# Edge tiles of a dilated attention with whole 128-row blocks

## The chip, the cores and the metric

The kernel runs on one core of one Trainium2 chip. The metric is the device time of one execution in microseconds (us); less is better. The time before is 2080.05 us, the median of three runs (2075.96 to 2084.55).

## The reference, cut to what matters

The layer normalises x (2048 tokens of 1024 channels), projects it, runs a state-space branch and an attention branch beside each other, gates both and adds the result to x. The change lies in the attention alone. Each of 8 heads attends in three patterns (window, dilation) = (128, 1), (512, 4), (2048, 16), always 64 keys to either side on its own sub-sequence, and the patterns are merged by their log-sum-exp:

```python
valid = (jnp.abs(ki - qi) <= half) & (ki >= 0) & (ki < n)
s = jnp.einsum('nhbqd,nhbkd->nhbqk', qb, kb) * (1.0 / math.sqrt(D))
s = jnp.where(valid, s, NEG_INF)
m = jnp.max(s, axis=-1, keepdims=True)
p = jnp.where(valid, jnp.exp(s - m), 0.0)
den = jnp.sum(p, axis=-1, keepdims=True)
o = jnp.einsum('nhbqk,nhbkd->nhbqd', p, vb) / den
```

Keys before the first or after the last token of a sub-sequence do not exist, so a query tile at either edge has fewer keys than one in the middle.

## The kernel before

Three phases follow each other. `phase_a` (to about 1068 us) normalises, projects and runs the state space. `phase_b` (about 1094 to 1701 us) runs the attention, and beside it the remaining projections and the gated linear unit as filler. `phase_c` merges the branches and does the output projection.

`phase_b` (L1299) walks 80 steps, made by `attn_steps` (L934): for each of 4 head pairs hp, the patterns p = 1, 0, 2 in that order; p = 1 and p = 0 have 8 steps of two query tiles, p = 2 has 4 steps of four. A step is a two-head piece of work in three stages, and the loop issues stage one of step i, stage two of step i-1 and stage three of step i-2, with filler from `run` (L1278) after each:

- `attn_scores` (L950) loads q and v at the first step of a quad (four tiles) by DMA from the POOL queue (from SP for the first two quads), makes the scores S in PSUM, adds the mask into P in SBUF while it finds the row minimum (VectorE, L1003), and takes the exponential of P in place (ScalarE, L1007). P is a tile of a pool with two buffers a head.
- `attn_turn` (L1010) transposes P on TensorE, four blocks a head into one PSUM tile `pp` (L1019), and copies `pp` to SBUF tiles `t` (L1030 ScalarE, L1032 VectorE). `pp` has two buffers.
- `attn_values` (L1036) multiplies each transposed block with its block of v into `po` (L1048). At the end of a quad `po` is copied out (L1059), and after p = 2 `attn_merge` (L1078) joins the three patterns through small DMAs and the products `ab` (L1117 to L1122).

A query tile in the middle has 256 keys, two blocks of 128. The first and the last tile of a sub-sequence have 192: one block of 64 and one of 128. `q_tiles` (L880) lists them. For p = 1 every step holds one such tile (sub-sequences of four tiles, two a step); for p = 0 the first and the last of eight steps do; p = 2 has none. So 40 of the 80 steps are edge steps, ten a head pair. In an edge step the 64-key block is transposed into 64 rows of `pp`, copied apart from the three others (two copies a head, dealt to ScalarE and VectorE in turn by `self.ev_`), and multiplied as a matmul over 64 rows. Each product with v is two matmul records in the trace, so a step has sixteen of `po`, of which an edge step has four with 64 rows.

The kernel is written with a planner that sets the order of the instructions on each engine from a simulated timeline; dependencies alone bind it, so the order in the trace is not the order of the source.

Of the kernel before, what the change touches and what calls it, by code (L numbers as in the profile page):

```python
# [9 lines left out]
F32 = mybir.dt.float32  # L10
F32R = mybir.dt.float32r
I32 = mybir.dt.int32
AF = mybir.ActivationFunctionType
# [26 lines left out]
class Kern:  # L40
# [862 lines left out]
    def attn_setup(self, base, ctx, pctx):  # L903
        ap, R = self.pool, dict(ctx=ctx, side="right")
        self.op = ap("op", ctx=base, side="right")
        self.kp = ap("kp", **R)
        self.qa = ap("qa", bufs=2, **R)
        self.vp = ap("vp", bufs=2, **R)
        self.aw = ap("aw", bufs=2, **R)
        mp = ap("mk", **R)  # L910
        self.mg = ap("mg", **R)

        self.kh = [self.kp.tile([128, 2048], F32R, name=f"kh{h}") for h in range(2)]
        self.kl = [self.kp.tile([128, 2048], F32R, name=f"kl{h}") for h in range(2)]
        self.mk = {}
        for n in ("m2", "m1", "m3"):
            t = mp.tile(list(self.ins[n].shape), F32, name=n)
            self.nc.sync.dma_start(t, self.ins[n])
            self.mk[n] = t
        self.pS = ap("pS", bufs=3, space=PSUM, ctx=pctx)  # L920
        self.pT = ap("pT", bufs=2, space=PSUM, ctx=pctx)
        self.pO = ap("pO", bufs=1, space=PSUM, ctx=pctx)
        self.ev_ = 0
        self.O = [self.op.tile([128, 2048], F32, name=f"o{p}", tag=f"o{p}") for p in range(2)] + [None]

    def k_load(self, hp, r):
# [23 lines left out]
    def attn_scores(self, x):  # L950
        nc, mm, R, C = self.nc, self.mm, 2048, 512
        hp, p, quad, per, g = x["hp"], x["p"], x["quad"], x["per"], x["group"]
        tiles = self.tiles[p]
        if x["sub"] == 0:
            late = hp > 0 or p != 1 or quad > 1

            g["q"] = [self.qa.tile([128, 512], F32R, name=f"q{h}") for h in range(2)]
            for h in range(2):
                o = (8 * p + 2 * hp + h) * 2 * 64 * R + 512 * quad
                (nc.gpsimd if late else nc.sync).dma_start(f(g["q"][h]), at(self.QT, o, [[R, 128], [1, 512]]))  # L960

            v = g["v"] = self.vp.tile([128, 5, 128], F32, name="v")
            c0 = 128 * hp
            if p == 2:
                (nc.gpsimd if late else nc.sync).dma_start(v[:, :4], at(self.V, 512 * quad * C + c0, [[4 * C, 128], [C, 4], [1, 128]]))
            else:
                run = 8 if p == 0 else 32
                base, m0 = (0, 4 * quad) if p == 0 else (512 * quad, 0)
                for m in range(m0, m0 + 5):
                    j0, j1 = max(run * m - run // 2, 0), min(run * m + run // 2, 128)  # L970
                    rows = [[512 * C, 4], [C, 4 * (j1 - j0)]] if p == 0 else [[C, 4 * (j1 - j0)]]
                    (nc.gpsimd if late else nc.sync).dma_start(v[:(16 if p == 0 else 4) * (j1 - j0), m - m0],  # L972
                                                               at(self.V, (base + 4 * j0) * C + c0, rows + [[1, 128]]))
            if p == 2:
                self.st[2] = self.aw.tile([128, 2, 2, 4], F32, name="st2", bufs=3)
            elif quad == 0:
                self.st[p] = self.aw.tile([128, 2, 2, 16], F32, name="st")
        q, kh, kl = g["q"], self.kh, self.kl
        st = x["st"] = self.st[p]
        w = 512 // per  # L980
        S = [self.pS.tile([128, per, w], F32, name="s") for h in range(2)]
        x["P"] = [self.aw.tile([128, per, w], F32, name=f"p{h}") for h in range(2)]
        for i, t in enumerate(x["idx"]):
            qs = slice(128 * (t % 4), 128 * (t % 4) + 128)
            for h in range(2):
                c = 0
                for ko, kd, kn, _ in tiles[t][0]:
                    o_ = S[h][:, i, c:c + kn]
                    mm(o_, q[h][:, qs], vw(kh[h], ko, kd), start=True, stop=False)
                    mm(o_, q[h][:, qs], vw(kl[h], ko, kd), start=False, stop=True)  # L990
                    c += kn
        for h in range(2):
            for i, t in enumerate(x["idx"]):
                nk, mask = tiles[t][2], self.mk[tiles[t][1]]
                c = (t, 4 * (t % 4) + t // 4, t % 4)[p]
                least, o = st[:, 0, h, c:c + 1], 0
                for _, kd, kn, m0 in tiles[t][0]:
                    pt, sc, mk = x["P"][h][:, i, o:o + kn], S[h][:, i, o:o + kn], mask[:, m0:m0 + kn]
                    if kn == 64:
                        pt, sc, mk = vw(pt, 0, [[16, 4], [1, 16]]), vw(sc, 0, [[16, 4], [1, 16]]), vw(mask, m0, [[32, 4], [1, 16]])  # L1000
                    elif len(tiles[t][0]) == 2:
                        mk = mask[:, (m0 + 127) // 128 * 128:][:, :128]
                    self.marks["dve"] = nc.vector.tensor_tensor_reduce(pt, sc, mk, op0=OP.add, op1=OP.min, scale=-0.125,  # L1003
                                                                       scalar=least if o else 3e38, accum_out=least)
                    o += kn
                pt = x["P"][h][:, i, :nk]
                self.marks["act"] = nc.scalar.activation(pt, pt, AF.Exp, bias=st[:, 0, h, c:c + 1], scale=-1.0,  # L1007
                                                         accum_out=st[:, 1, h, c:c + 1])

    def attn_turn(self, x):  # L1010

        nc, tiles = self.nc, self.tiles[x["p"]]
        x["blocks"] = blocks = [(i, b, b * tiles[t][3][0][1], vt, n) for i, t in enumerate(x["idx"])
                                for b, (vt, n) in enumerate(tiles[t][3])]
        x["T"] = []
        for h in range(2):
            pp = self.pT.tile([128, 4, 128], F32, name="pp")
            for c, (i, b, o, vt, n) in enumerate(blocks):
                self.tr(pp[:n, c], x["P"][h][:, i, o:o + n], self.ident)  # L1019
            ts = self.aw.tile([128, 4, 128], F32, name=f"t{h}")  # L1020
            rows = [y[4] for y in blocks]
            c = 0
            while c < 4:
                e = c
                while e < 4 and rows[e] == rows[c]:
                    e += 1
                o_, i_ = ts[:rows[c], c:e], pp[:rows[c], c:e]
                self.ev_ += 1
                if self.ev_ % 2:
                    nc.scalar.activation(o_, i_, AF.Copy)  # L1030
                else:
                    nc.vector.tensor_copy(o_, i_)  # L1032
                c = e
            x["T"].append(ts)

    def attn_values(self, x):  # L1036
        nc, mm, R = self.nc, self.mm, 2048
        hp, p, quad, per, g = x["hp"], x["p"], x["quad"], x["per"], x["group"]
        tiles = self.tiles[p]
        if x["sub"] == 0:  # L1040
            g["po"] = self.pO.tile([128, 4, 128], F32, name="po")
            if p == 2:
                g["o2"] = self.op.tile([128, 512], F32, name="o2", bufs=3)
        po, v, O = g["po"], g["v"], self.O
        for c, (i, b, o, vt, n) in enumerate(x["blocks"]):
            last = b == len(tiles[x["idx"][i]][3]) - 1
            for h in range(2):
                mm(po[64 * h:64 * h + 64, per * x["sub"] + i], v[:n, vt, 64 * h:64 * h + 64], x["T"][h][:n, c],  # L1048
                   start=b == 0, stop=last)
        if x["sub"] < 4 // per - 1:  # L1050
            return
        if p == 0:
            o_ = vw(O[0], 32 * quad, [[8, 4], [128, 16], [1, 8]])
        elif p == 1:
            o_ = vw(O[1], 512 * quad, [[32, 4], [128, 4], [1, 32]])
        else:
            o_ = g["o2"].rearrange("p (a j) -> p a j", a=4)
        i_ = po if p == 2 else po.rearrange("p m (s j) -> p m s j", s=16 if p == 0 else 4)
        (nc.scalar.copy if quad % 2 else nc.vector.tensor_copy)(o_, i_)  # L1059
        if p == 2:  # L1060
            self.merges.append(self.attn_merge(hp, quad, x["st"], g["o2"]))
        elif quad == 3:
            self.merges.append(self.attn_stats(hp, p, x["st"]))
# [435 lines left out]
```

## Time and profile before

| | before |
|---|---|
| median of three runs | 2080.05 us |
| the profiled execution | 2084.98 us |
| its span, first to last instruction | 2083.2 us |
| TensorE matmul busy | 1975.6 us, 95% |
| TensorE weight load busy | 1764.6 us, 85% |
| VectorE busy | 1292.2 us, 62% |
| ScalarE busy | 725.7 us, 35% |
| GpSimd busy | 826.8 us, 40% |
| mean granted TensorE clock | 0.974 |
| chain of work that ended last | TensorE 59%, VectorE 16%, DMA 13% |

The profiled execution took 1.9 us more than its span and 0.24% more than the median. PE is TensorE's matmuls and PEld its weight loads, DVE is VectorE, ACT ScalarE, POOL GpSimd, SP SyncE. A form such as `128*64` on PE gives the rows and the columns of the array that the instruction uses. Matmuls are pipelined and their ends are modelled, so the distance between two starts says more of TensorE's pace than the duration of one.

### The profile page before, as it was taken

Reading aid. Unit: us, or ns where it says so; the run is one execution under the profiler, and the core shown is the slowest. Engines: PE = TensorE matmul, PEld = TensorE weight load, DVE = VectorE, ACT = ScalarE, POOL = GpSimd, SP = SyncE. Lnnn points to the kernel's source line nnn. Section 1 sums busy time; section 2 is a strip of 40 time slices with the busy share of each in tenths; the row PEclk is TensorE's granted clock in tenths of the full one; section 3 lists DMA queues with packets and bytes.
Section 4 is the critical chain, followed back from the end, with each engine's and each line's share of the span. In section 5 each row is a group of like instructions: output and inputs, shape, how many; then the busy total and the mean of one; then the engine's idle time right before and its main releaser. Section 6 shows DMA issues by size and latency. Waiting matters only on the chain.

```text
span 2083.2 us, 37578 instructions
## 1 busy us (share of the span) xinstructions
PE 1975.6 (95%) x13612; PEld 1764.6 (85%) x13612; DVE 1292.2 (62%) x3312; ACT 725.7 (35%) x1829; POOL 826.8 (40%) x1088
## 2 busy tenths in 40 slices
PE   6899999999999999899989999998998978999999
PEld 6788899998788889899977877876887978899997
DVE  8867575978566778587755455455567655433432
ACT  4221343333232343233326544554655632100110
POOL 4310464538636654475442346346345222000000
PEclk9999999999999999999999999999998998999999
DMA  5632464445533444634474465566676547433332
GB/s 192 195 100 73 126 198 147 121 120 158 166 109 114 153 144 141 178 114 133 130 230 138 154 180 165 166 178 179 208 204 179 161 134 233 147 114 115 117 111 76
DMA packets 272059, 312.54 MB, mean 150 GB/s; under 512 B 86594, under 2 KB 182226, under 8 KB 271874
## 3 DMA queue, kind: packets, MB, share of 16 engines
q1 hardware_dynamic: 250914, 260.39, 41.8%
q0 software_dynamic: 20960, 49.76, 8.1%
q8 instruction: 107, 1.75, 0.3%
q14 instruction: 78, 0.64, 0.1%
HBM read 202.12 MB, written 105.71 MB: 148 GB/s over the span
## 4 chain that ended last, share of the span: by engine, by line
PE 59%; DVE 16%; DMA 13%; SPq 4%; issue 3%; POOL 3%; ACT 2%; DVEq 0%; ACTq 0%; POOLq 0%
PE acc L53 39%; PE po L53 12%; PE s L53 3%; PE pp L56 3%; DMA raw<-in_w_in 2%; DVE wlo L311 2%; DMA ab<-AL 2%; SPq L513 1%; DVE zs L843 1%; DMA AL<-e 1%; DMA ACTA<-fth 1%; DVE zs L841 1%; DMA s<-ST 1%; PE y L53 1%; SPq L1111 1%
## 5 line engine op out<-in xcount | busy, mean ns | idle before, releaser
L53 PE MATMUL acc<-xh,whi 128*128 128x512 f32 (+1 forms) x960 | 376.7, 393 | 17.8 <-DVE xsc L379 8.3
L53 PE MATMUL acc<-whi,xh 128*128 128x256 f32 x1280 | 368.2, 288 | 2.9 <-ACT qr L451 2.1
L53 PE MATMUL acc<-xl,whi 128*128 128x512 f32 (+1 forms) x960 | 367.9, 384 | 1.1 <-DVE xl L208 1.1
L53 PE MATMUL acc<-xh,wlo 128*128 128x512 f32 (+1 forms) x960 | 367.3, 384 | 0.0
L53 PE MATMUL acc<-whi,xl 128*128 128x256 f32 x1280 | 364.7, 285 | 1.9 <-POOL xl L263 1.6
L53 PE MATMUL acc<-wlo,xh 128*128 128x256 f32 x1280 | 364.7, 285 | 0.0
L53 PEld LDWEIGHTS acc<-whi,xh 128*128 128x128 f32 x1280 | 247.9, 194 | 5.6 <-ACT qr L451 2.4
L53 PEld LDWEIGHTS acc<-whi,xl 128*128 128x128 f32 x1280 | 247.9, 194 | 2.5 <-POOL xl L263 1.9
L53 PEld LDWEIGHTS acc<-wlo,xh 128*128 128x128 f32 x1280 | 248.1, 194 | 0.0
L53 PEld LDWEIGHTS acc<-xh,whi 128*128 128x128 f32 x960 | 184.9, 193 | 54.0 <-issue 10.9
L1007 ACT ACTIVATE p<-p,st 128x256 f32<-128x256 f32 (+2 forms) x384 | 172.8, 452 | 143.6 <-DVE st L1003 143.2
L311 DVE TENSOR_TENSOR wlo<-raw,whi 128x512 fp32r<-128x512 f32 x168 | 151.2, 918 | 110.9 <-ACT whi L310 110.1
L53 PEld LDWEIGHTS acc<-xh,wlo 128*128 128x128 f32 x960 | 184.9, 193 | 33.7 <-issue 0.5
L53 PEld LDWEIGHTS acc<-xl,whi 128*128 128x128 f32 x960 | 185.4, 193 | 29.4 <-DVE xl L208 1.6
L310 ACT ACTIVATE whi<-raw 128x512 fp32r<-128x512 f32 x176 | 102.9, 625 | 165.7 <-DMA raw<-in_w_in 140.1
L1003 DVE CUSTOM_DVE_ANT_0 p<-s,m 128x256 f32<-128x256 f32 (+2 forms) x376 | 115.8, 358 | 68.3 <-PE s L53 45.0
L972 POOL DMA_DIRECT2D v<-V x150 | 91.7, 618 | 121.2 <-PE po L53 115.0
L53 PE MATMUL s<-kh,q 128*128 128x256 f32 (+2 forms) x400 | 104.3, 299 | 12.1 <-DVE st L1003 7.2
L53 PE MATMUL acc<-pair,wsh 128*128 128x256 f32 x512 | 99.3, 295 | 16.3 <-DVE cm L1373 11.4
L53 PE MATMUL po<-t,v 128*64 128x128 f32 (+1 forms) x1280 | 110.3, 293 | 1.8 <-ACT t L1030 0.9
L56 PE MATMUL pp<-c_ident,p 128*128 128x128 f32 (+1 forms) x640 | 94.1, 281 | 13.5 <-DVE t L1032 12.4
L53 PEld LDWEIGHTS po<-t,v 128*64 128x64 f32 (+1 forms) x1280 | 75.3, 141 | 37.2 <-issue 23.7
(331 smaller groups left out, 4392.1 us busy)
## 6 DMA issues: line engine op xcount, KB each, us to landing
raw<-in_w_in SPq DMA_DIRECT2D x176, 256.0 KB
q<-QT POOLq DMA_DIRECT2D x92, 256.0 KB, 4.2
ab<-AL SPq DMA_DIRECT2D x96, 128.0 KB
ug<-U SPq DMA_DIRECT2D x128, 64.0 KB
GA<-th SPq DMA_DIRECT2D x32, 256.0 KB
GB<-th SPq DMA_DIRECT2D x32, 256.0 KB
raw<-GB SPq DMA_DIRECT2D x32, 256.0 KB
xres<-in_x SPq DMA_DIRECT2D x32, 256.0 KB
```

Of the source, the lines that this page charges most:

```text
L53: return self.nc.tensor.matmul(*a, **k)
L56: return self.nc.tensor.transpose(*a)
L310: self.nc.scalar.activation(hi, t, AF.Copy)
L311: (eng or self.nc.vector).tensor_sub(lo, t, f(hi))
L513: nc.sync.dma_start(at(dst, d, e), f(t[64 * h:64 * h + 64]))
L841: V.tensor_tensor_scan(zs[:64, n, 2:258], r[:64].to_broadcast([64, 256]), z[:64, n], 0.0, op0=OP.mult, op1=OP.add)
L843: V.tensor_tensor_scan(zs[64:, n, 0:256][:, ::-1], r[64:].to_broadcast([64, 256]), z[64:, n, ::-1], 0.0, op0=OP.mult, op1=OP.add)
L972: (nc.gpsimd if late else nc.sync).dma_start(v[:(16 if p == 0 else 4) * (j1 - j0), m - m0], at(self.V, (base + 4 * j0) * C + c0, rows + [[ ...
L1003: self.marks["dve"] = nc.vector.tensor_tensor_reduce(pt, sc, mk, op0=OP.add, op1=OP.min, scale=-0.125, scalar=least if o else 3e38, accum_ ...
L1007: self.marks["act"] = nc.scalar.activation(pt, pt, AF.Exp, bias=st[:, 0, h, c:c + 1], scale=-1.0, accum_out=st[:, 1, h, c:c + 1])
L1111: nc.sync.dma_start(t[64 * h:64 * h + 64], at(self.AL, hp * 6 * R + p * 2 * R + h * R + 512 * r, [[0, 64], [1, 512]]))
```

## The change

It makes every block of an edge step 128 rows. The half block of v gets its other 64 rows filled with zeros by GpSimd, each time that v is loaded for a quad with an edge (40 fills of 64x128 in all). P lies in four fixed tiles, two steps by two heads, which VectorE clears once at the start of the attention, so that what stands beyond the 192 keys is always a finite number, and the zeros in v take it out of the product. All four transposes of a head then fill 128 rows, one copy a head moves `pp` to `t`, on ScalarE for one head and on VectorE for the other, and all sixteen matmuls of a step run over 128 rows.

```diff
@@ attn_setup
         self.ev_ = 0
+        self.P = [[self.aw.tile([128, 512], F32, name=f"p{h}{i}", bufs=1) for h in range(2)] for i in range(2)]
+        for t in self.P[0] + self.P[1]:
+            self.nc.vector.memset(t, 0.0)
+        self.turn_ = 0
@@ attn_scores
                     j0, j1 = max(run * m - run // 2, 0), min(run * m + run // 2, 128)
+                    if j1 - j0 < run:
+                        nc.gpsimd.memset(v[64:, m - m0], 0.0)
...
-        x["P"] = [self.aw.tile([128, per, w], F32, name=f"p{h}") for h in range(2)]
+        self.turn_ += 1
+        x["P"] = [t.rearrange("p (i w) -> p i w", i=per) for t in self.P[self.turn_ % 2]]
@@ attn_turn
-                self.tr(pp[:n, c], x["P"][h][:, i, o:o + n], self.ident)
+                self.tr(pp[:, c], x["P"][h][:, i, o:o + 128], self.ident)
             ts = self.aw.tile([128, 4, 128], F32, name=f"t{h}")
-            rows = [y[4] for y in blocks]
-            c = 0
-            while c < 4:
-                e = c
-                while e < 4 and rows[e] == rows[c]:
-                    e += 1
-                o_, i_ = ts[:rows[c], c:e], pp[:rows[c], c:e]
-                self.ev_ += 1
-                if self.ev_ % 2:
-                    nc.scalar.activation(o_, i_, AF.Copy)
-                else:
-                    nc.vector.tensor_copy(o_, i_)
-                c = e
+            self.ev_ += 1
+            if self.ev_ % 2:
+                nc.scalar.activation(ts, pp, AF.Copy)
+            else:
+                nc.vector.tensor_copy(ts, pp)
             x["T"].append(ts)
@@ attn_values
-                mm(po[64 * h:64 * h + 64, per * x["sub"] + i], v[:n, vt, 64 * h:64 * h + 64], x["T"][h][:n, c],
+                mm(po[64 * h:64 * h + 64, per * x["sub"] + i], v[:, vt, 64 * h:64 * h + 64], x["T"][h][:, c],
                    start=b == 0, stop=last)
```

## Rows read from the trace of the kernel before

**Rows 1.** Stretches: us, then busy PE, PEld, DVE, ACT, POOL; granted clock; DMA share, GB/s.

```profile
1068.00:1094.00 26.00, 20.48 (x94) 16.85 (x93) 4.10 (x13) 5.02 (x13) 3.23 (x4) 0.88 0.88 291
1094.00:1250.00 156.00, 151.65 (x1048) 119.93 (x1048) 78.73 (x333) 84.16 (x293) 57.54 (x93) 0.98 0.54 157
1250.00:1400.00 150.00, 144.15 (x1005) 115.72 (x1003) 75.85 (x297) 73.47 (x257) 74.84 (x104) 0.99 0.59 172
1400.00:1550.00 150.00, 142.70 (x1092) 122.38 (x1091) 93.59 (x330) 84.21 (x278) 72.27 (x102) 0.95 0.64 191
1550.00:1701.00 151.00, 134.01 (x1152) 121.59 (x1148) 103.20 (x315) 82.87 (x259) 60.11 (x72) 0.95 0.57 158
```

**Rows 2.** Groups by form, 1094-1701 us (busy us, mean ns | idle before): products, transposes.

```profile
L53 PE MATMUL po<-t,v 64*64 64x128 f32 x160 | 21.4, 310 | 0.4 <-DVE o L1059 0.4
...
L56 PE MATMUL pp<-c_ident,p 128*128 128x128 f32 x560 | 86.7, 280 | 3.6 <-DVE t L1032 2.5 <-DVE sr L1085 1.1
...
L56 PE MATMUL pp<-c_ident,p 128*64 128x128 f32 x80 | 22.9, 287 | 9.9 <-DVE t L1032 9.9
...
L56 PEld LDWEIGHTS pp<-c_ident,p 128*128 128x128 f32 x560 | 67.3, 143 | 14.5 <-DVE t L1032 4.0 <-DVE sr L1085 1.6 <-issue 1.4
...
L56 PEld LDWEIGHTS pp<-c_ident,p 128*64 128x64 f32 x80 | 9.0, 112 | 14.3 <-DVE t L1032 11.6 <-issue 1.7 <-DVE ft L1153 0.3
```

**Rows 3.** Timeline of PEld, an edge step, then one of whole blocks (start, duration).

```profile
1117.27 0.20 PEld L53 LDWEIGHTS po<-t,v 64*64 64x64 f32 x4 [0.20 <-issue]
1117.63 0.64 PEld L53 LDWEIGHTS po<-t,v 128*64 128x64 f32 x12 [0.17 <-issue]
1118.44 0.39 PEld L56 LDWEIGHTS pp<-c_ident,p 128*64 128x64 f32 x4 [0.17 <-DVE t L1032]
1119.00 0.13 PEld L53 LDWEIGHTS po<-t,v 128*64 128x64 f32 x1 [0.17 <-issue]
...
1166.82 0.86 PEld L56 LDWEIGHTS pp<-c_ident,p 128*128 128x128 f32 x8 [0.17 <-issue]
1167.84 0.85 PEld L53 LDWEIGHTS po<-t,v 128*64 128x64 f32 x16 [0.17 <-issue]
1168.87 0.19 PEld L53 LDWEIGHTS s<-kl,q 128*128 128x128 f32 x1 [0.17 <-issue]
```

**Rows 4.** Groups by form, 1094 to 1701 us: the copies of transposes.

```profile
L1032 DVE COPY t<-pp 128x512 f32<-128x512 f32 x40 | 27.5, 688 | 23.7 <-PE pp L56 23.6
...
L1032 DVE COPY t<-pp 128x384 f32<-128x384 f32 x40 | 21.4, 547 | 2.8 <-ACT t L1030 2.7
...
L1032 DVE COPY t<-pp 64x128 f32<-64x128 f32 x40 | 10.8, 277 | 11.4 <-ACT t L1030 11.0
L1030 ACT ACTIVATE t<-pp 64x128 f32<-64x128 f32 x40 | 9.8, 260 | 8.5 <-PE pp L56 5.7 <-PE po L53 2.8
```

**Rows 5.** Who waited for whom, 1094 to 1701 us: total, times, longest.

```profile
POOL v L972 <- PE po L53: 115.0, 24, 12.2
DVE ab L1120 <- DMA ab<-AL: 35.2, 9, 6.2
DVE p L1003 <- PE pp L56: 16.3, 12, 3.7
DVE t L1032 <- ACT t L1030: 13.6, 16, 2.2
```

**Rows 6.** Timeline around a stall of the transposes, at a p = 1 step of hp 1.

```profile
1270.51 0.69 DVE L1120 TENSOR_TENSOR ab<-ab,o 128x512 f32<-128x512 f32 x1 [5.30 <-DMA ab<-AL]
...
1271.12 2.94 DVE L311 TENSOR_TENSOR wlo<-raw,whi 128x512 fp32r<-128x512 f32 x2
...
1273.98 0.47 DVE L1032 COPY t<-pp 64x128 f32<-64x128 f32 x2
1274.31 1.06 PE L56 MATMUL pp<-c_ident,p 128*64 128x128 f32 x8 [2.36 <-DVE t L1032]
```

**Rows 7.** Groups by form, whole span: the fills of constants.

```profile
L678 POOL MEMSET bbp<- 128x256 f32 x2 | 0.6, 328 | 0.0
...
L715 DVE MEMSET T<- 128x16 f32 x4 | 0.3, 72 | 2.9 <-POOL ww L140 2.9
```

## The prediction

> **What bounds the kernel now.** I read the busy time by stretch first [rows 1]. The change lies between 1094 and 1701 us, and there the matmul engine is the one to look at: in the four stretches its matmuls cover 151.65, 144.15, 142.70 and 134.01 us of 156, 150, 150 and 151, so 34.5 us of 607 are idle. VectorE (78.73 to 103.20 us), ScalarE and GpSimd are busy for 37% to 68% of each. A microsecond of VectorE or ScalarE is therefore worth something only where a stall of the matmuls hangs on it, while a microsecond that TensorE itself needs less is worth nearly a microsecond, because the filler beside the attention and the whole of phase c follow on the same engine.
>
> The second view is the groups by form [rows 2], which says how many edge steps there are (160 matmuls of 64 rows, four a step: 40 steps) and what stands before their instructions. The third is the timeline of the weight loads [rows 3], read for the distance between starts. The fourth is the waits [rows 5], to see what a copy of the transposes holds up.
>
> **The products with v.** In [rows 3] a step of whole blocks starts its sixteen products at 1167.84 and the next work starts at 1168.87: 1.03 us. An edge step starts four products over 64 rows at 1117.27, twelve over 128 rows at 1117.63, and the next work at 1118.44: 1.17 us for the same sixteen. The engine takes a pause whenever it goes from one use of the array to another; entering and leaving the group costs the same in both, and the edge step has one such change more, inside the group. The difference is 0.14 us. The forms with 64 rows vanish with the change, and with them 40 x 0.14 = 5.6 us. Bounds: 0, if the planner already keeps the two forms apart in every step (a group that stands alone has an entry and an exit with either form), and 2 x 5.6 = 11.2, if every step had a change in and one back. I take 5.6: the rows show one change a step.
>
> Does the wider contraction cost anything? Inside the group, the first four products take 1117.63 - 1117.27 = 0.36 us with the change of form; less 0.14 that is 0.22. The twelve take 0.81 with the exit, the sixteen 1.03, so four whole-row products are 1.03 - 0.81 = 0.22. A product over 64 rows is no faster than one over 128: cost 0. The Trainium skill speaks against the change here: "TensorEngine Tiling (Array Packing)", section When to Use Tiling, has it that a contraction of 64 allows two row tiles, so up to twice the pace, which padding gives up. The trace disagrees for this kernel, 0.22 against 0.22; by the page's rule the forty groups of four would have been worth 0.11 us each, and the sum would be 5.6 - 4.4 = 1.2 us of gain.
>
> **The transposes.** 80 of 640 grow from 64 to 128 columns of weights. Their load goes from a mean of 112 to 143 ns, their matmul from 287 to 280 [rows 2]. In [rows 3] four of them take 0.56 us until the next work, and eight with 128 columns 1.02, both with one exit, so the pace differs by nothing that can be seen: (1.02 - 0.56) / 4 = 0.115 us each, and 0.56 less four of these leaves a pause of 0.10 as elsewhere. I take 0; the upper bound, were the loads bare, is 80 x 31 ns = 2.5 us. The lower is 0, since the matmul's columns are the same. "TensorE: Matmul & The Clock Gate", section LDWEIGHTS (loading the stationary operand), of the Trainium skill makes the load grow with its columns, which by its figure is an estimate of 53 ns each, 4.3 us in all; put in the path, that would leave 1.3 us of the gain. The row shows 31 ns, and under cover of the matmuls.
>
> **The copies.** VectorE loses 40 copies of 64x128 at 277 ns and 40 of 128x384 at 547, and gains 40 of 128x512 at 688 [rows 4]: 11.1 + 21.9 - 27.5 = 5.5 us less work. ScalarE loses as many instructions. Before, the two copies of one head went to two engines and came one after the other: 13.6 us of VectorE's waiting ends with ScalarE's copy of the same tile [rows 4, 5]. This wait goes. What is late next is mostly VectorE's wait for a DMA or for the scores, so I count no gain on the path for it, except for the stalls of the matmuls that end with a VectorE copy: before the edge transposes 9.9 us of idle are put down to it [rows 2]. [Rows 6] shows one. VectorE waits 5.30 us for a merge's DMA, then does the merge and two weight splits, and only at 1273.98 the copies that free `pp`; the matmuls lose 2.36 us. With the change the first head's copy is ScalarE's and free of that queue, but the second head's still stands in it, now 0.69 us instead of two of 0.24 each. The first four transposes (0.46 us) can go early, then the same wait follows. I take 0 of the 9.9; the bounds are 9.9 gained and, for a copy that is longer by 0.69 - 0.47 = 0.22 us at each of 40 steps, 8.8 lost.
>
> **P in fixed tiles.** Two tiles a head before, two after, so VectorE's write of P in step i waits for the transposes of step i-2 either way. That wait costs VectorE 16.3 us in 12 times [rows 5] and stays. Queued behind it on VectorE are copies and merges, behind those the transposes. Bounds: it may go (16.3 us of VectorE) or double; neither reaches the matmuls as long as they have filler. The four clearing instructions: the trace has a VectorE fill of 128x16 at 72 ns [rows 7], and a 128x512 copy at 688 [rows 4]; four lie between 0.3 and 2.8 us. I take 2 us, in the stretch 1068 to 1094 where VectorE is busy for 4.10 of 26 us [rows 1]: hidden. Without that cover it is 2 us at the start of the attention.
>
> **The zeros in v.** 40 fills of 64x128 on GpSimd; the nearest row is 128x256 at 328 ns [rows 7], so 0.1 to 0.33 us each, 4 to 13 us in all; I take 8. GpSimd is busy for 265 of 607 us [rows 1]. The fill needs the same thing as the v load behind it, the last product of the quad that held the buffer (115.0 us of waiting already [rows 5]), so no new release is waited for. Behind it stand the loads of v and q and the merge's products, each later by a few tenths. The quads are loaded ahead, and no idle time of any size before the products in [rows 2] comes from there: 0 on the path, 13 us if all of it were bare.
>
> **The sum** is -5.6 us: 2084.98 becomes 2079.4 in the profiled execution. That execution ran 4.93 us above the median of 2080.05; set against the median it is 2074.4 us, and I forecast 2074.
>
> **The rivals.** First, *the copies do reach the path*: the lockstep between ScalarE and VectorE goes, VectorE comes to `pp` earlier, and the 9.9 us vanish too. For it speaks that these stalls stand before edge transposes alone; against it, that the row behind one [rows 6] is a DMA and not a copy. Time: 2080.05 - 5.6 - 9.9 = 2064.5; after idle time the clock is lower, and were the 0.05 that the last two stretches lack [rows 1] (15 us) given back in the same share, 9.9 of 24.3 us idle there, another 6 us: 2058.
>
> Second, the other side: *the second head's copy is late as a whole*. Every edge step's second copy is now one instruction of VectorE, and VectorE's order has the merge's product before it that waits for a DMA, 35.2 us in nine times [rows 5]. Today the matmuls lose 2.36 of 5.30 us [rows 6], because filler covers the rest. If the planner puts the product ahead of the copy and less filler between, they lose all: 2.9 us more at each of nine, 26 us, less 5.6: 2101; at half of them 2088. It decides from the point where over two of the nine lose their cover. For it: the planner does not know when the DMA lands. Against it: the first head's tile no longer hangs on VectorE.
>
> Third, *the change gives nothing*: all queues of the phase are planned anew, with 80 copies fewer and 44 fills more, and groups of products split by other work cost as much as the changes of form that went. A group of its own costs an entry and an exit; some 40 more of them, at 0.14, and the time is 2080.
>
> **How the numbers follow.** The forecast 0.55 (its own range 2068 to 2079), the first rival 0.20, the second 0.12, the third 0.13. A measurement of this kernel can tell about 0.5%, 10.4 us: the bounds are 2069.65 and 2090.45. Faster: the first rival and a little of the forecast's low end, 0.26. Slower: most of the second, 0.10. Same: 0.64. The range, 2058 to 2090, takes in the first rival and the second to half its price.
>
> **What would show it.** No 64-row products and no 64-column transposes of P; sixteen products in 1.03 us at an edge step; 80 copies fewer, 40 on either engine and none of VectorE's waits for ScalarE's copy; matmul idle time before transposes about as long as now. The forecast is wrong if that idle time moves by more than 5 us either way, if the groups of products are cut into more pieces, or if the products wait for GpSimd.

## The result, and the profile after

The changed kernel takes 2057.89 us (median of four runs, 2052.14 to 2058.54) where the kernel before took 2079.56: the ratio is 0.9899, with a 95% interval of 0.9877 to 0.9920. It is 22 us, 1.0%, faster. The forecast was 2074, so the sign was right, but the gain it had was a quarter of what came. The measured median lies 0.1 us below 2058, the lower end of the stated range; as a ratio it is 0.9899 of 2080.05, which is 2059.0.

The profiled execution of the changed kernel took 2057.8 us, 27.2 less than that of before. Not all of that is the change's. Up to the first scores of the attention the engines' orders of matmuls are the same in both kernels; the next rows give the last filler matmul and the first scores, of the kernel before and then of the changed one (start, duration):

```profile
1085.30 0.39 PE L53 MATMUL acc<-xh,wlo 128*128 128x512 f32 x1
1090.63 0.50 PE L53 MATMUL s<-kh,q 128*128 128x192 f32 x1 [4.94 <-DMA v<-V]
```

```profile
1080.45 0.39 PE L53 MATMUL acc<-xh,wlo 128*128 128x512 f32 x1
1087.58 0.50 PE L53 MATMUL s<-kh,q 128*128 128x192 f32 x1 [6.74 <-DMA v<-V]
```

The changed kernel's execution was 4.85 us ahead before anything differed (the orders of VectorE and GpSimd part at 1082 us, with the fills), and 3.05 us ahead at the first scores. Up to that last filler matmul the clock records of the two traces have TensorE at the lower of its two levels, 1.2 GHz, for 44 us before and for 38 us after, so an estimate of 3.4 of the 4.85 us is the clock's. What is left from the first scores on, 24 us, is about the 22 of the medians.

Busy time by stretch of the changed kernel (columns as in [rows 1]; the attention ends at 1664 us instead of 1693):

```profile
1068.00:1094.00 26.00, 19.26 (x89) 16.61 (x87) 7.10 (x27) 5.49 (x15) 1.79 (x6) 0.80 0.86 278
1094.00:1250.00 156.00, 152.40 (x1102) 124.02 (x1101) 79.19 (x319) 83.56 (x284) 65.84 (x113) 1.00 0.54 156
1250.00:1400.00 150.00, 146.92 (x1039) 120.47 (x1039) 79.73 (x316) 79.42 (x266) 82.00 (x123) 0.99 0.65 188
1400.00:1550.00 150.00, 145.91 (x1197) 128.89 (x1196) 100.18 (x348) 91.97 (x295) 79.57 (x118) 0.98 0.72 209
1550.00:1665.00 115.00, 106.09 (x924) 98.87 (x923) 73.59 (x235) 63.59 (x196) 38.87 (x50) 0.96 0.55 155
```

Against [rows 1] the matmuls are idle for 19.7 us from 1094 us to the attention's end, where it was 34.5 to 1701 (some 4 of these 34.5 behind the attention's end at 1693), and the granted clock is higher in the third and the last stretch (0.98 and 0.96 after 0.95 and 0.95). So idle time went and clock came back, which the forecast had at nothing. From the first scores to the end of the execution, the matmuls are busy for 13.4 us less (939.8 to 926.4) and idle for 10.7 us less, which makes up the 24. Of the 13.4, the array form is 5.6 by the forecast's price. TensorE stood at 1.2 GHz for 62 us of this stretch before and for 50 after, so the clock is an estimate of at most 5.8 us more.

The groups by form of the whole span, answering to [rows 2, 4, 7] (count, busy us, mean ns, idle before; six rows of a longer list):

```profile
L53 PE MATMUL po<-t,v 128*64 128x128 f32 x1280 | 97.4, 282 | 0.0
L56 PE MATMUL pp<-c_ident,p 128*128 128x128 f32 x640 | 92.8, 279 | 10.7 <-DVE t L1032 5.0 <-ACT t L1030 2.7 <-DVE sr L1084 2.4
L1032 DVE COPY t<-pp 128x512 f32<-128x512 f32 x80 | 54.9, 687 | 22.9 <-PE pp L56 22.6
L1030 ACT ACTIVATE t<-pp 128x512 f32<-128x512 f32 x80 | 46.5, 582 | 6.4 <-PE pp L56 5.7 <-PE po L53 0.5
L976 POOL MEMSET v<- 64x128 f32 x40 | 8.2, 210 | 60.5 <-PE po L53 39.9 <-DMA ZB<-th 15.4 <-issue 4.7
L926 DVE MEMSET p<- 128x512 f32 x4 | 1.9, 485 | 8.7 <-DMA zb<-ZB 8.5
```

All forms are whole: 1280 products over 128 rows, 640 transposes of 128 columns, 80 copies on either engine instead of 120. And the weight loads of an edge step, answering to [rows 3]:

```profile
1110.90 0.85 PEld L53 LDWEIGHTS po<-t,v 128*64 128x64 f32 x16
1111.93 0.42 PEld L56 LDWEIGHTS pp<-c_ident,p 128*128 128x128 f32 x4 [0.17 <-ACT p L1014]
```

Sixteen products in 1.03 us instead of 1.17, as forecast.

### The profile page after: what moved, and what is told of

Same layout as the page of the kernel before. It is cut to its first block, busy times and chain, and to the rows that moved or that the text cites. A ratio compares the mean times of both kernels' runs of the same rounds, so it can differ in the third digit from the quotient of the medians.

```text
span 2056.0 us, 37526 instructions
## 1 busy us (share of the span) xinstructions
PE 1960.6 (95%) x13612; PEld 1762.9 (86%) x13612; DVE 1283.1 (62%) x3276; ACT 722.2 (35%) x1789; POOL 838.7 (41%) x1128
## 4 chain that ended last, share of the span: by engine, by line
PE 62%; DVE 15%; DMA 12%; SPq 3%; POOL 3%; issue 3%; ACT 2%; DVEq 0%; POOLq 0%; ACTq 0%
PE acc L53 42%; PE po L53 11%; PE s L53 3%; PE pp L56 3%; DVE wlo L311 2%; DMA ab<-AL 2%; DMA raw<-in_w_in 1%; DMA ACTA<-fth 1%; DMA raw<-in_w_out 1%; PE y L53 1%; DMA AL<-e 1%; DVE zs L843 1%; DMA ST<-sr 1%; PE tp L56 1%; DVE zs L841 1%
## 5 line engine op out<-in xcount | busy, mean ns | idle before, releaser
L53 PE MATMUL s<-kh,q 128*128 128x256 f32 (+3 forms) x400 | 105.4, 301 | 15.5 <-DVE st L1010 8.6
L53 PE MATMUL acc<-pair,wsh 128*128 128x256 f32 x512 | 100.1, 297 | 15.3 <-DVE cm L1372 10.7
L53 PE MATMUL s<-kl,q 128*128 128x256 f32 (+3 forms) x400 | 103.1, 297 | 0.0
L56 PE MATMUL pp<-c_ident,p 128*128 128x128 f32 x640 | 92.8, 279 | 10.7 <-DVE t L1032 5.0
L53 PEld LDWEIGHTS acc<-pair,wsh 128*128 128x128 f32 x512 | 86.0, 205 | 17.3 <-issue 6.4
```

The costliest lines, as they stand in the source:

```text
L53: return self.nc.tensor.matmul(*a, **k)
L56: return self.nc.tensor.transpose(*a)
```

## The experiments

The theory at this point had two parts: the array form is worth 5.6 us, and the copies reach the path (the first rival), which is worth the other 16. Its rival: the planner set all queues of the attention anew, and the 16 us are this plan's luck. Twelve kernels were run, each beside the kernel before on the same chip. Each has a plan of its own, since any edit makes the planner order the queues again.

**One part alone.** First, one copy a head without whole products:

```diff
+        x["P"] = [t.rearrange("p (i w) -> p i w", i=per) for t in self.P[self.turn_ % 2]]
...
-                self.tr(pp[:n, c], x["P"][h][:, i, o:o + n], self.ident)
+                self.tr(pp[:, c], x["P"][h][:, i, o:o + 128], self.ident)
...
+            self.ev_ += 1
+            if self.ev_ % 2:
+                nc.scalar.activation(ts, pp, AF.Copy)
+            else:
+                nc.vector.tensor_copy(ts, pp)
...
```

> Fixed P, whole transposes and one copy a head, but the products with v keep their 64-row blocks and v gets no zeros. If the copies carry the 16 us that the forecast did not have, this is about 16 us faster than before (2064) and still has the 40 changes of array form, groups of sixteen products at 1.17 us. If the whole products carry it, it is within 2 us of before (2078 to 2080). If the order of the planner carries it, the time is anywhere between 2058 and 2085 and the idle time of the matmuls between 1094 and 1701 us follows it.

Measured: 0.9977 of before (0.9966 to 0.9988), 5 us faster. The matmuls' waits for these copies in the attention (total, times, longest):

```profile
PE pp L56 <- DVE t L1030: 8.7, 4, 3.4
PE pp L56 <- ACT t L1028: 2.2, 3, 1.0
```

Second, whole products, with fixed P and whole transposes too, and the copies still in two parts:

```diff
+                        nc.gpsimd.memset(v[64:, m - m0], 0.0)
...
+                self.tr(pp[:, c], x["P"][h][:, i, o:o + 128], self.ident)
...
-                o_, i_ = ts[:rows[c], c:e], pp[:rows[c], c:e]
+                o_, i_ = ts[:, c:e], pp[:, c:e]
...
-                mm(po[64 * h:64 * h + 64, per * x["sub"] + i], v[:n, vt, 64 * h:64 * h + 64], x["T"][h][:n, c],
+                mm(po[64 * h:64 * h + 64, per * x["sub"] + i], v[:, vt, 64 * h:64 * h + 64], x["T"][h][:, c],
```

> Fixed P, whole transposes, zeros in v and products over 128 rows everywhere, but two copies a head in the edge steps as before. If only the changes of array form count here, 5.6 us faster than before (2074), with 13 us of VectorE waiting for ScalarE's copies as before. If the copies are without weight, about as fast as the changed kernel (2058).

Measured: 0.9938 (0.9921 to 0.9955), 13 us faster. The same waits, and VectorE's wait for ScalarE's copies:

```profile
PE pp L56 <- DVE t L1039: 17.0, 8, 5.9
PE pp L56 <- ACT t L1037: 0.2, 1, 0.2
DVE t L1039 <- ACT t L1037: 15.3, 16, 2.2
```

So this kernel gained 13 us while its copies held the matmuls up for 17.2 us; one copy a head had brought that to 10.9.

Third, the fixed P tiles alone:

```diff
+        self.P = [[self.aw.tile([128, 512], F32, name=f"p{h}{i}", bufs=1) for h in range(2)] for i in range(2)]
...
-        x["P"] = [self.aw.tile([128, per, w], F32, name=f"p{h}") for h in range(2)]
+        x["P"] = [t.rearrange("p (i w) -> p i w", i=per) for t in self.P[self.turn_ % 2]]
```

> Only the fixed, cleared P tiles: the same products, transposes and copies as before. By the theory of the copies and by that of the products 2080, within 2 us of before. If the wait on P's tiles (VectorE behind the transposes, 16.3 us before) is what went, several us faster. If the planner's order decides, off by more than 5 us to either side.

Measured: 1.0013 (0.9999 to 1.0027), 3 us slower and at most 6, so fixed tiles alone bring no gain here. Against this base the one copy, with whole transposes, is worth 7.5 us (1.0013 - 0.9977, of 2076), and the whole products, with whole transposes too, 15.6. The parts add up to what all of them brought together, 2.7 - 7.5 - 15.6 = -20.4, but each of these times comes from one plan. And 15.6 is 10 us more than the array form explains, and the 16 us expected of the copies did not come. Either a change of array form costs far more than 0.14 us, or plans differ.

**The price of an array form.** The next kernel doubles the changes: the two blocks of an edge tile are multiplied in the other order, so the 64-row products stand between others.

```diff
-        for c, (i, b, o, vt, n) in enumerate(x["blocks"]):
+        order = [c for t in range(per) for c in ([e for e, y in enumerate(x["blocks"]) if y[0] == t])[::-1 if any(y[0] == t and y[4] == 64 for y in x["blocks"]) else 1]]
+        seen = {}
+        for c in order:
+            i, b, o, vt, n = x["blocks"][c]
+            b = seen[i] = seen.get(i, -1) + 1
```

> The kernel before with the two blocks of every edge tile multiplied in the other order, so that the 64-row products of a step stand between 128-row products: two changes of array form inside a step's products in place of one, the rest of the work the same. If a change costs 0.14 us and no more, 40 more of them make it 5.6 us slower (2081 where the kernel before takes 2076). If the changes carry the whole 15 us that whole products brought, about 15 us slower (2091).

Measured: 1.0026 (1.0011 to 1.0042), 5.4 us slower. In its timeline of weight loads an edge step reads:

```profile
1191.68 0.42 PEld L53 LDWEIGHTS po<-t,v 128*64 128x64 f32 x8 [0.37 <-issue]
1192.27 0.19 PEld L53 LDWEIGHTS po<-t,v 64*64 64x64 f32 x4 [0.17 <-issue]
1192.64 0.20 PEld L53 LDWEIGHTS po<-t,v 128*64 128x64 f32 x4 [0.17 <-issue]
1193.01 0.19 PEld L53 LDWEIGHTS acc<-xh,whi 128*128 128x128 f32 x1 [0.17 <-issue]
```

The sixteen products take 1.33 us with two changes inside, 1.17 with one [rows 3], 1.03 with none. So 0.14 to 0.16 us is the price, and forty of them are 5.6 us. It holds over the whole attention. Between its products the kernel before has 41 changes of form and this one 82; at the higher clock two products stand 0.20 us apart, from start to start, where the form changes between them, and 0.06 us on the average where it does not. The time agrees, 5.4 us, but as one plan it could not fix the price by itself. The other 10 us of whole products, and 16 of the changed kernel, are something else.

**The same work under other plans.** One constant sets how much filler the loop asks for ahead of the first step. Moving it by a few microseconds leaves the work alone and makes the planner place the whole attention anew. The kernel before and the changed one were each run with 24, 26 and 28 us in place of 25:

```diff
-LEAD, PACE, P2, TAIL, WSAT, EVERY = 25.0, (1.1, 1.05, 1.0), 1.0, 8.0, 3, 3
+LEAD, PACE, P2, TAIL, WSAT, EVERY = 26.0, (1.1, 1.05, 1.0), 1.0, 8.0, 3, 3
```

> The kernel before with one constant of the filler's pacing nudged (26 us of filler ahead of the first step in place of 25): same work, another plan. If times follow from the work that the change removes, within 2 us of before. If the plan decides how long the matmuls stall in the attention, it differs from before by 5 us or more, and that is the spread against which the gain of 22 us has to be read.

> The changed kernel with the same nudge of the filler as in the nudged kernel before (26 us ahead of the first step in place of 25). If the gain follows from the work, 2055 to 2060, 0.8% to 1.1% under the kernel before. If a lucky plan made the changed kernel, it loses 5 us or more of the 22.

> The kernel before with 24 us of filler ahead of the first step in place of 25; a third plan of the same work. If plans spread the time by several us, it lies 3 to 8 us off the kernel before, to either side; its pair tells more.

> The changed kernel with 24 us. If only the array form's 5.6 us belong to the work, and the other 16 us of the gain were this plan's luck, the pair differs by about 6 us, give or take the plans' spread of some 5. If 14 us (the pair without simulated timeline) or more belong to the work, by 14 or more.

> The kernel before with 28 us of filler ahead of the first step, a fourth plan. As for 24: a few us off the kernel before.

> The changed kernel with 28 us. Against its pair about 6 us less if the gain of the work is the array form alone, 14 us or more if the stalls that went belong to the work too.

And both were run with the planner's simulated timeline switched off:

```diff
-    with tile.TileContext(nc, schedule_with_timeline_sim=True) as tc:
+    with tile.TileContext(nc, schedule_with_timeline_sim=False) as tc:
```

> The kernel before with the planner's simulated timeline switched off, so that another rule sets the order of each engine's instructions; same work. No forecast for its time against the kernel before (5 to 60 us slower seems likely, since the filler's place is then another); it is the base for its pair.

> The changed kernel with the planner's simulated timeline switched off as well. If the gain belongs to the work, it is about 20 us faster than its pair. If it belongs to how the simulated timeline happened to place things, the two differ by the array form's 5.6 us alone.

Measured, as ratios to the kernel before on the same chip with their 95% intervals; the difference of a pair is that of its two ratios, in us of the kernel before, known to some 5 us either way. The two kernels of the 26 us plan ran on different chips, each beside the kernel before:

| plan | kernel before | changed kernel | changed less before |
|---|---|---|---|
| 25 us (as given) | 1 | 0.9899 (0.9877 to 0.9920) | -21 us |
| 24 us | 1.0010 (0.9992 to 1.0027) | 0.9943 (0.9924 to 0.9962) | -14 us |
| 26 us | 0.9989 (0.9978 to 1.0000) | 0.9982 (0.9966 to 0.9999) | -1 us |
| 28 us | 1.0052 (1.0035 to 1.0069) | 0.9988 (0.9969 to 1.0006) | -13 us |
| no simulated timeline | 1.0729 (1.0713 to 1.0744) | 1.0666 (1.0650 to 1.0682) | -13 us |

The same work spreads over 13 us (0.63%) in the kernel before and over 18 us (0.89%) in the changed one, among four plans each, and the intervals of the extremes lie apart. The given plan is the best of the changed kernel's four. The five pairs have a mean of -12.5 us. So of the 22 us measured, about 9 were this plan's and 12.5 come with the change in the mean: 5.6 of the array form and some 7 more. These 7 are not well known. The five pairs lie between -1 and -21 us, which leaves their mean open by some 9 us to either side (95%), and without the given plan, whose gain the others were to test, the mean of the other four is -10.4.

**Where the rest may come from.** The waits of the matmuls in the attention (total, times, longest), of the kernel before and then of the changed kernel:

```profile
PE pp L56 <- DVE t L1032: 18.5, 9, 3.4
PE s L53 <- DVE st L1003: 7.2, 2, 6.3
PE s L53 <- DMA v<-V: 4.9, 1, 4.9
PE pp L56 <- ACT t L1030: 1.3, 1, 1.3
```

```profile
PE s L53 <- DVE st L1010: 8.6, 2, 8.0
PE s L53 <- DMA v<-V: 6.7, 1, 6.7
PE pp L56 <- DVE t L1032: 5.0, 3, 3.1
PE pp L56 <- ACT t L1030: 2.7, 1, 2.7
```

Transposes that wait for a copy to free `pp` lose 19.8 us before (18.5 + 1.3) and 7.7 after. That these waits shrink holds beyond the one plan. Read the same way, the eight kernels with two copies a head have 15.3 to 22.5 us of it, 18.7 in the mean; the six with one copy have 6.1 to 18.8, 11.6 in the mean. The pair without simulated timeline shows it, before and then after:

```profile
PE pp L56 <- DVE t L1032: 22.5, 12, 4.8
PE acc L53 <- DVE fth L1192: 18.1, 5, 11.4
PE s L53 <- DVE st L1003: 12.1, 5, 3.5
```

```profile
PE acc L53 <- DVE fth L1191: 22.5, 6, 12.1
PE pp L56 <- DVE t L1032: 13.7, 5, 4.5
...
PE s L53 <- DVE st L1010: 8.2, 3, 3.6
PE pp L56 <- ACT t L1030: 5.1, 4, 3.8
```

22.5 us of waiting for copies became 18.8 (13.7 + 5.1). The waits for copies fell in all five pairs. The matmuls' idle time in the attention fell in three of them and grew in two, where the matmuls waited longer for something else:

| plan | waits for copies, before and changed | idle time, before and changed |
|---|---|---|
| 25 us (as given) | 19.8, 7.7 us | 30.7, 20.3 us |
| 24 us | 15.3, 6.1 | 38.4, 22.6 |
| 26 us | 20.2, 16.2 | 26.8, 36.1 |
| 28 us | 21.7, 10.1 | 35.3, 37.0 |
| no simulated timeline | 22.5, 18.8 | 70.4, 64.7 |

The waits for copies fell by 8.1 us in the mean, the idle time by 4.2. So one copy a head does shorten the waits for copies; that the time followed is argued and not shown. One more thing goes with the single copy: the products come in fewer unbroken runs (110 became 102 under the given plan, and 115, 106, 111 and 83 became 101, 93, 94 and 80 under the others; 100 with one copy alone, 112 with whole products alone). Eleven runs fewer in the mean, with a change of form on either side of each at 0.09 to 0.14 us, are an estimate of 2 to 3 us.

With one copy a head the first head's tile hangs on ScalarE alone and the second's on VectorE alone; with two, either tile hung on both, and VectorE waited for ScalarE besides [rows 5]. In the kernel before without simulated timeline that wait was

```profile
DVE t L1032 <- ACT t L1030: 28.7, 21, 2.2
```

and none of the six kernels with one copy has it.

**And the 26 us plan, which gives nothing.** The changed kernel under that plan:

```profile
PE acc L53 <- DVE fth L1191: 11.1, 5, 9.5
PE pp L56 <- DVE t L1032: 10.3, 5, 5.2
PE pp L56 <- ACT t L1030: 5.9, 7, 3.2
PE pp L56 <- DVE sr L1084: 4.0, 3, 2.2
```

Transposes still lose 16.2 us to copies, and the filler's matmuls lose 11.1 us, 9.5 of it in one place, to a VectorE product of the gated linear unit (fth, L1191). The kernel before under the 26 us plan has no wait for fth in the attention, and one of 2.9 us behind it. This is read from one execution of each; why the product came late was not tried.

## Why the prediction was right or wrong, point by point

- **The array form, 5.6 us**: right. The step of the timeline went to 1.03 us, twice the changes inside the products cost 0.14 to 0.16 us a step more, and the time of that kernel, 5.4 us slower (2.3 to 8.7), agrees.
- **The wider contraction, 0**: right. Sixteen products over 128 rows take 1.03 us in the edge step that was changed as in the whole step of [rows 3].
- **The transposes, 0**: right. The mean matmul is 279 ns, where the two forms had 280 and 287 [rows 2]. The working had a wrong reading, though: the four transposes at 1118.44 in [rows 3] are merged under the form of the first, and three of them have 128 columns. Taken singly over the attention, the matmul after a transpose of either form starts 0.11 us behind it (medians), so the 0 stands.
- **The zeros in v, 4 to 13 us of GpSimd and 0 on the path**: right. 40 fills took 210 ns each, 8.2 us, and no product waited for GpSimd. The clearing of P took 1.9 us where 2 were taken.
- **P in fixed tiles, 0**: right within what one plan can tell, +2.7 us (-0.2 to +5.6).
- **The copies, 0 of the 9.9 us of stalls**: wrong. This is the step that failed, and by the sign that the prediction had set for being wrong, more than 5 us of change in the matmuls' idle time before transposes, the forecast failed with it (20.9 us before, 10.7 after). It argued from one stall [rows 6] that the second head's copy still stands behind the merge, so the wait stays. It does stay in places (3.1 us once in the changed kernel), but over the attention these waits fell from 19.8 to 7.7 us, and the mean over all kernels from 18.7 to 11.6. One row was taken for all nine waits. The 9.9 us are the wait before the transposes of 64 columns alone; with the others it is 18.5 us for VectorE's copies, 6.2 of it before small transposes of `st`, so these stalls did not stand before edge transposes only, as the first rival had it. And the wait of VectorE for ScalarE (13.6 us [rows 5]) was counted as no gain on the path, though it lies in the order of VectorE ahead of the copies that free `pp`. The first rival had this mechanism, with 2064.5 us, and with the clock that comes back 2058. That the measured time falls on the 2058 is in part luck: by the pairs, some 9 us of it were this plan's.
- **The plan**: a term that the sum did not have. The third rival named the new plan, but only as a way to lose the gain, with 0.13. Plans of the same work lie up to 13 and 18 us apart; a forecast for this kernel needs some 8 us to either side for that alone. Under the 26 us plan the third rival's time is what came, but not by its mechanism: the products were not cut into more runs there (106 before, 93 changed).
- **The second rival**, a late second copy, did not come: no kernel with one copy loses more to copies than its pair.

The mean of the five pairs, 12.5 us, would have been 2067.5 us: nearer to the first rival's 2064.5 than to the forecast, though at 9 us to either side it rules out neither.

## What to carry to other kernels

Here a narrow form of matmul amid wide ones cost more than the rows it saved (0.14 us a change, and nothing saved): price the change of form by the distance between starts, and pad with zeros where the padding is free. A small copy on a second engine is not free because it is small: it ties a buffer to two queues, and the buffer is free when the slower one is done. Where a planner orders the queues, a gain of 1% cannot be put down to the edit from one plan: nudge a harmless constant in both kernels and compare pairs.

## What the runs showed of the hardware that was not expected

A change between 128 and 64 rows of the array cost 0.14 to 0.16 us each time (1.03, 1.17 and 1.33 us for the same sixteen products), while a transpose with 64 columns of weights between transposes with 128 cost nothing that can be seen (0.11 us from start to start either way). Two executions of the same matmuls were 4.85 us apart after 1080 us, which is nearly as much as the array form is worth.
